# Block 2's adaLN vectors in a two-block transformer kernel: from GpSimd's products and sums to TensorE's column tiles

## The chip, the cores and the metric

The kernel runs on one core of one Trainium2 chip. The metric is the time of the whole program on the device, in microseconds (us): the median of three runs. Weights lie in HBM and are streamed to SBUF during the run; all data are fp32, some products run in fp32r halves or fp16.

## The reference

Two transformer blocks on 256 tokens of 1024 features. Block 1 ends in a layer of product-key experts ("PEER": 16384 experts in 128 rows of 128, each with a key `expert_u` and a value `expert_v`); block 2 has two layers, the second with routed experts. Each layer of block 2 starts from vectors that depend on the condition `c_2` alone:

```python
for l in range(DEPTH_2):                              # 2 layers
    mod = jax.nn.silu(c) @ ada_w[l] + ada_b[l]        # [1, 1024] @ [1024, 6144]
    sh1, sc1, g1, sh2, sc2, g2 = jnp.split(mod[:, None, :], 6, axis=-1)
    h = rmsnorm(x, ln1_g[l]) * (1.0 + sc1) + sh1
    ...
```

So 2 x 1024 x 6144 weights (48 MB) are read once and multiplied by one vector. In block 1 the experts' half computes, for every row of 128 experts, gelu(keys x h), times a weight for each expert and token (zero for those not chosen), times the values.

## The kernel before, in words

The kernel is one Python class `B`; its methods emit instructions in a program order, many as generators whose steps are woven together. The tile framework then puts them in order for each engine (by priority in program order, with a simulated timeline) and adds the waits; each engine and SP's queue then follow that order.

**The weights' stream.** `Ring` (L65) holds slots of 1 MB; a slot's DMA is issued on SP's queue as soon as the slot's last reader has been emitted (L98, and L96 for keys that come as four sources). `split` (L274 to 288) makes two fp32r halves of a weight tile: ScalarE copies the high one `whi` (L284), VectorE subtracts for `wlo` (L288). `mm3` (L404 to 409) is three TensorE products of such halves.

**The expert rows.** `peer` (L1327) works through 128 rows. T: the row's keys transposed, from row 32 on by VectorE (`peer_tv`, L1246: transposes L1254, ScalarE's copy `uth` L1255, VectorE's subtraction `utl` L1256). A: keys times h, 24 products of 256 columns (`peer_a`, L1295), gelu on ScalarE (L1301). W: the weights of the next group of 32 rows, a 32nd part beside each row (`peer_w_steps`, L1195): VectorE makes masks O2, eq, O1 (L1207 to 1209), TensorE eight small products (L1217), ScalarE and VectorE put them into W (L1222, L1223). g: weights times gelu on VectorE (L1310), its high half gh on ScalarE (L1312) and the remainder gl on GpSimd (L1313). Y: values times g, twelve products of 512 columns (`peer_y`, L1318). The key products of rows 0 to 31 run ahead while the experts are chosen; rows 96 to 127 have no next W. In rows 0 to 6 `group_steps` (L1259) also lays h out anew with banks of PSUM tag t.

**adaLN.** `mods` is one tile [128, 512]: value 512 j + i of a group of 2048 is at partition 32 j + r, column i, where r is the row of the group. Block 1's three groups come from `ada_steps` (L308): for each of eight chunks of 128 weight rows (1 MB, [128, 2048]) four products, one for each j, of a [128, 32] stationary operand that is zero but for one silu column, into partitions 32 j to 32 j + 31 of a PSUM bank. The zero columns put the sums into row r alone. Groups 1 and 2 go through `aring`, a ring with one slot. After eight chunks VectorE adds the bank to `mods` (L318).

Block 2's six groups come from `ada2_steps` (L321), in 96 steps of half a MB: 256 columns and half of the 1024 weight rows, into one half of a tile [128, 2, 4, 256] in the same slot as `aring`. On GpSimd: a product with the silu column (`c2`, L195; L348), two sums (L350; L352 and L353) into an accumulator `ada` (three buffers). When both halves are summed, TensorE multiplies the 256 columns by a column of ones (`pick`, L337), which sums over partitions; after eight such products VectorE adds the bank to `mods` (L340). The bank is of tag t, of which there are two.

**The order around it.** `self.ada(1)` (L1408) advances `ada2_steps` by one step in every second row of rows 0 to 31 and in each row after them; a step's DMA waits for GpSimd's work on the half before last. Rows 97, 104, 109 and 116 also emit the constants of block 2 and, at row 116, `prep2`, which reads the first of the new vectors. Banks of PSUM: four of tag acc (the sums Y), two of w, two of t.

Of the kernel before, what the change touches and what calls it, by code (L numbers as in the profile page):

```python
# [27 lines left out]
# block 2: chunks of w_in (z) and w_out (w), and the steps beside them  # L28
# [36 lines left out]
class Ring:  # L65
    """Slots of 1 MB that the weights stream through in the order of their use."""
# [6 lines left out]
    def grow(self, pool, n, tag="ring", until=None):  # L73
        """n more slots, for the entries before number until."""
        for _ in range(n):
            self.free.append((pool, n, tag, until))
        self._issue()

    def add(self, key, view, shape):
        """view: the source, or a list of sources for 32 partitions each with the first of them."""  # L80
        self.plan.append((key, view, shape))
# [21 lines left out]
    start = _issue  # L103
# [8 lines left out]
    def done(self):  # L112
        """The last instruction that reads the slot taken longest ago has been emitted."""
        self.free.append(self.inflight.popleft())
        self._issue()


def kchunk(w, k0, nk, c0, ncol):
    """Rows k0*128.. of a matrix [rows, cols] as [128, nk, ncol]."""
    return w[k0 * 128:(k0 + nk) * 128, c0:c0 + ncol].rearrange("(k p) c -> p k c", p=128)  # L120


class B:
# [27 lines left out]
    def splits(self, cx, n):  # L151
        """n more buffers for the parts of split weights while cx is open."""
        p = cx.enter_context(self.pool("split"))
        self.sps = self.sps + [(p, n)] * n
        cx.callback(self.unsplit, p)
# [4 lines left out]
    def rings(self, cx, n, until=None):  # L160
        """n more slots of the weights' ring, for the entries before number until."""
# [7 lines left out]
    # vectors laid as rows of 128, transposed to columns  # L169
# [18 lines left out]
    def vectors_T(self):  # L188
# [6 lines left out]
        self.c2 = self.cp.tile([128, 8], F32, name="c2")       # silu(c_2)  # L195
        nc.scalar.activation(self.c2, c2, AF.Sigmoid)
        nc.vector.tensor_tensor(self.c2, self.c2, c2, op=ALU.mult)
# [15 lines left out]
    def ln_stats(self, x, name="ln"):  # L213
        """mean and rstd of the rows of [128, 1024]."""
# [9 lines left out]
    def ln_norm(self, dst, x):  # L224
        """dst = (x - mean) * rstd."""
# [5 lines left out]
    def rms_norm(self, dst, x, g=None):  # L231
        """dst = x * rsqrt(mean of x^2 + eps) [* g]."""
# [13 lines left out]
    def modT_steps(self, *jobs):  # L246
        """For each job: hi/lo [128 d, 8, tok] = the transposed xn [128 tok, 2, 1024] * scale[d] + shift[d], in two parts.
        The first step needs xn alone."""
# [23 lines left out]
    def split(self, src, shape, tag="w", eng=None):  # L272
        """src as an fp32r high part and the fp32r rest."""
# [18 lines left out]
    # Value 512 j + i of a group of 2048 values is at partition 32 j + r, column i of mods, where r is the group's row:  # L292
    # 0..2 of block 1's three groups for the latent, 3 of the first for the context, 6 + 3 l + g in block 2.
# [12 lines left out]
    def ada_steps(self, g):  # L306
        """mods += the products of block 1's vectors with a group's weights; one step per 1 MB."""
# [13 lines left out]
    def ada2_steps(self):  # L321
        """The same for block 2, 256 columns and half of the rows a step: GpSimd sums over the rows that share a partition."""
        nc = self.nc
        parts = [(l, g, c, a) for l in range(2) for g in range(3) for c in range(8) for a in range(2)]
        slots = self.prep_pool.tile([128, 2, 4, 256], F32, tag="aring", name="ada2")
        accs, p = {}, None
        for n in range(len(parts) + 5):
            if n < len(parts):
                l, g, c, a = parts[n]
                nc.sync.dma_start(out=slots[:, n % 2], in_=kchunk(self.I["ada_w_2"][l], 4 * a, 4, 2048 * g + 256 * c, 256))  # L330
            if n % 2 == 0 and n >= 6:
                l, g, c, _ = parts[n - 6]
                r = 6 + 3 * l + g
                if p is None:
                    p = self.bank("t")
                j = 32 * (c // 2)
                nc.tensor.matmul(p[j:j + 32, 256 * (c % 2):256 * (c % 2) + 256], self.pick[:, 11 - r:43 - r], accs.pop(n // 2 - 3),  # L337
                                 start=True, stop=True)
                if c == 7:
                    nc.vector.tensor_tensor(self.mods, p, self.mods, op=ALU.add)  # L340
                    p = None
            if 1 <= n <= len(parts):
                i = n - 1
                w, a = slots[:, i % 2], i % 2
                if a == 0:
                    accs[i // 2] = self.pp.tile([128, 256], F32, tag="ada", name="ada", bufs=3)
                acc = accs[i // 2]
                nc.gpsimd.tensor_tensor(w, w, bcast(self.c2[:, 4 * a:4 * a + 4].rearrange("p (k o) -> p k o", o=1), (128, 4, 256)),  # L348
                                        op=ALU.mult)
                nc.gpsimd.tensor_tensor(w[:, 0:2], w[:, 0:2], w[:, 2:4], op=ALU.add)  # L350
                if a:
                    nc.gpsimd.tensor_tensor(acc, acc, w[:, 0], op=ALU.add)  # L352
                nc.gpsimd.tensor_tensor(acc, acc if a else w[:, 0], w[:, 1], op=ALU.add)  # L353
            yield
# [5 lines left out]
    def silu_cols(self):  # L360
        """silu of c and c_ctx as columns 2 and 5 of cs1, the rest zero."""
# [13 lines left out]
        self.pick = self.cp.tile([128, 43], F32, name="pick")     # ones in column 11  # L375
# [6 lines left out]
    def mod_cols(self, dst, r0, n, tag="t"):  # L382
        """dst [128, n, 16]: columns of the groups r0.. ."""
# [7 lines left out]
    def row_bcast(self, dst, r, js, scale=1.0, tag="t"):  # L391
        """dst [128, 512 * len(js)]: values 512 j.. of group r on every partition."""
# [11 lines left out]
    def mm3(self, o, ah, al, bh, bl, start, stop):  # L404
        """o += (ah + al)^T (bh + bl) without the product of the two rests."""
# [5 lines left out]
    def mm3u(self, o, wh, wl, kk, n):  # L411
        """mm3 with the first n of u's tokens (latent, then context); the first product clears the whole bank's marks."""
# [7 lines left out]
    def proj_steps(self, c0, n, res):  # L420
        """Features on partitions: res[ct] = [128 features, n tokens] of the 2 column tiles."""
# [14 lines left out]
    def projT_steps(self, c0, res, order=((0, (0, 1, 2, 3)), (1, (0, 1, 2, 3)))):  # L436
        """Tokens on partitions: res[tt] = [128 tokens, 256 features] of the 4 token tiles; order is the steps'
        half of the features that are summed over and token tiles."""
# [18 lines left out]
    def proj_lr(self):  # L457
        """The two gate ranks: partitions 96.. of a bank [128, 512 tokens]."""
# [8 lines left out]
    def hg_bounds(self):  # L467
        """max(lb, floor) and 1 - lb as columns [128, (direction, head)]."""
# [16 lines left out]
    def hg_gate(self, d, pr, banks):  # L485
        """Keys and decays of the latent and the context, [128, 2, 256] each."""
# [21 lines left out]
    def gla_gates(self, lr):  # L508
        """exp(logsigmoid / 16) of both directions: latent and context decays [128, 2, 256]."""
# [24 lines left out]
    def ctx_state(self, hpp, d, kc, fc, vc, res, rest=1):  # L534
        """End state [128 (dk of both groups' heads), 2, 128 dv] of the context in direction d."""
        nc = self.nc
        E = self.mt("E", (2, 256), 2)
        if d == 0:     # products of the later decays, by doubled blocks
# [15 lines left out]
        else:          # products of the earlier decays  # L554
# [22 lines left out]
        S = self.mt(f"S{d}", (2, 2, 128), 2)   # [dk of both heads, g, r, dv], zero where dk is the other head's  # L577
# [8 lines left out]
    # In blocks of 2 h tokens, the forward direction's keys of the first half meet the queries of the second half, the  # L586
    # backward direction's keys of the second half the queries of the first. A: a key's decays up to the halves' border;
    # P: a query's from the border. One doubling of h extends both by the other half's whole decay.
    def level_arrays(self, h, q, ks, A, P):
        """X of both directions [128, 2, 256]: keys times A in one half of each block, queries times P in the other."""  # L590
# [29 lines left out]
    def mix_steps(self, hpp, q, ks, fs, v, S, res):  # L620
        """o of the batch's heads in two banks of [128 tokens, heads x 128]."""
# [4 lines left out]
        Psb = self.mt("Psb", (4, 512))     # index 2 r + g for head hpp g + r  # L626
# [98 lines left out]
        # head norms  # L725
# [17 lines left out]
    def mix_out(self, o, h0, base, permuted, gain, gates):  # L743
        """Gain and gate; features base.. of the transposed mix in two parts, from heads h0, h0 + 1 of o."""
# [40 lines left out]
    def block1_mix(self, after):  # L785
        """The mixed tokens times w_out, in 4 banks; after(banks) runs while the mixer's memory is still held."""
        nc, I, tc = self.nc, self.I, self.tc
        O = self.WIN
        with ExitStack() as cx:
# [44 lines left out]
            back = []      # context states under way  # L834
# [43 lines left out]
            # the second mixer's parts  # L878
# [71 lines left out]
    def wout_steps(self, key, hi, lo, res):  # L950
        """[256 tokens, 1024] = (hi + lo)^T w in 4 banks (token tile, column half); the last chunk token tile by tile."""
# [1344 lines left out]
```

## Time and profile before

| | |
|---|---|
| time, median of 3 runs (all) | 2951.28 us (2951.82, 2949.05, 2951.28) |
| profiled execution: span on the core | 2951.2 us (no separate time for it) |
| mean granted TensorE clock | 0.950 |
| PE busy | 2671.7 us (91%) |
| VectorE (DVE) busy | 2475.4 us (84%) |
| ScalarE (ACT) busy | 1558.4 us (53%) |
| GpSimd (POOL) busy | 1006.3 us (34%) |
| HBM read | 616.18 MB, 209 GB/s over the span |

PE is TensorE's products, PEld its weight loads, SP the queue that issues most DMAs. L12 is line 12 of the kernel. An fp32 product shows as two records, each of the product's columns. A busy PE is not PE at its peak: the end of a product is modelled and a record overlaps the next; the pitch from start to start is what a product takes from the engine. The granted clock is a share of full speed (2.4 GHz is 1.0).

### The profile page before, as it was taken

To read this page: it belongs to the slowest core of one execution; us is meant where nothing else is said; L and a number is where in the kernel's file an instruction comes from. 1 tells how busy PE (TensorE), PEld (TensorE's weight loads), DVE (VectorE), ACT (ScalarE), POOL (GpSimd) and SP (SyncE) were. 2 spreads that over 40 slices of the span, in tenths; PEclk is the share of its full clock that TensorE was granted. 3 is DMA by queue.
4 is the path that set the end of the run, shared out by engine and by line. 5 is a ranking of instruction groups with operands and counts; after the bars stand their busy time and mean duration, and the time that the engine had idled before them with its cause. 6 is when DMAs were issued, how large, how long until landed. Compare 5 with 4: busy or idle time off the path is not lost. (4 is left out here: it accounts for less than half of the span.)

```text
span 2951.2 us, 45631 instructions
## 1 busy us (share of the span) xinstructions
PE 2671.7 (91%) x17417; PEld 2278.4 (77%) x17417; DVE 2475.4 (84%) x3850; ACT 1558.4 (53%) x2296; POOL 1006.3 (34%) x818
## 2 busy tenths in 40 slices
PE   6999796978898888888988899998999999999997
PEld 4878686956677777767877899987878778777775
DVE  4668799999899999999766754576999999999987
ACT  3244453433333333335446544475777777777775
POOL 2564353577677778776211100010000000000010
PEclk8999898989889999999998999998999999999999
DMA  7543442234666666667753455435999999999993
GB/s 256 199 147 102 152 138 84 101 107 157 179 182 170 189 171 193 178 181 203 184 182 104 133 179 180 142 126 178 348 338 352 339 342 350 335 344 342 338 333 146
DMA packets 341733, 620.28 MB, mean 210 GB/s; under 512 B 14755, under 2 KB 184633, under 8 KB 338433
## 3 DMA queue, kind: packets, MB, share of 16 engines
q1 hardware_dynamic: 340256, 616.06, 63.6%
q8 instruction: 138, 2.26, 0.3%
q0 software_dynamic: 1072, 0.82, 0.1%
q14 instruction: 91, 0.74, 0.1%
q10 hardware_dynamic: 176, 0.40, 0.0%
HBM read 616.18 MB, written 1.05 MB: 209 GB/s over the span
## 5 line engine op out<-in xcount | busy, mean ns | idle before, releaser
L288 DVE TENSOR_TENSOR wlo<-ring,whi 128x1024 fp32r<-128x1024 f32 x785 | 1027.1, 1329 | 235.9 <-ACT whi L284 230.5
L284 ACT ACTIVATE whi<-ring 128x1024 fp32r<-128x1024 f32 x785 | 822.6, 1058 | 520.2 <-PE acc L409 171.7
L2190 POOL TENSOR_TENSOR x<-x,moeroom 128x512 f32<-128x512 f32 x30 | 53.8, 1809 | 848.2 <-DVE moeroom L2189 848.2
L408 PE MATMUL acc<-wlo,xh 128*128 128x512 f32 x768 | 307.8, 401 | 2.8 <-DVE wlo L288 2.6
L407 PE MATMUL w<-hh,uth 128*128 128x256 f32 x1024 | 305.2, 298 | 4.4 <-DVE W L1223 1.4
L409 PE MATMUL acc<-whi,xl 128*128 128x512 f32 x768 | 304.0, 396 | 0.2 <-DVE xl L2133 0.2
L409 PE MATMUL w<-hh,utl 128*128 128x256 f32 x1024 | 300.7, 294 | 3.1 <-POOL utl L1243 3.1
L407 PE MATMUL acc<-whi,xh 128*128 128x512 f32 x768 | 301.4, 399 | 0.7 <-ACT xh L2132 0.7
L408 PE MATMUL w<-hl,uth 128*128 128x256 f32 x1024 | 298.9, 292 | 0.0
L348 POOL TENSOR_TENSOR ada<-ada,c 128x1024 f32<-128x1024 f32 x96 | 210.6, 2197 | 99.6 <-DMA ada<-in_ada_w_dram 99.4
L408 PE MATMUL acc<-wlo,gh 128*128 128x512 f32 x512 | 208.8, 418 | 25.7 <-DVE wlo L288 25.7
L407 PEld LDWEIGHTS w<-hh,uth 128*128 128x128 f32 x1024 | 204.7, 200 | 16.4 <-issue 3.1
L407 PE MATMUL acc<-whi,gh 128*128 128x512 f32 x512 | 192.0, 413 | 26.9 <-ACT gh L1312 26.8
L1256 DVE TENSOR_TENSOR utl<-ut,uth 128x512 fp32r<-128x512 f32 x192 | 188.3, 1016 | 28.2 <-ACT uth L1255 28.1
L409 PEld LDWEIGHTS w<-hh,utl 128*128 128x128 f32 x1024 | 203.5, 199 | 4.0 <-POOL utl L1243 3.8
L408 PEld LDWEIGHTS w<-hl,uth 128*128 128x128 f32 x1024 | 203.8, 199 | 3.1 <-issue 0.2
L409 PE MATMUL acc<-whi,gl 128*128 128x512 f32 x512 | 190.8, 433 | 9.3 <-POOL gl L1313 9.3
L1217 PEld LDWEIGHTS <-O 128*128 128x128 f16 x1024 | 117.5, 148 | 82.2 <-issue 48.9
L1255 ACT ACTIVATE uth<-ut 128x512 fp32r<-128x512 f32 x192 | 111.4, 622 | 128.5 <-PE w L408 86.6
L408 PEld LDWEIGHTS acc<-wlo,xh 128*128 128x128 f32 x768 | 144.6, 188 | 42.7 <-DVE wlo L288 7.6
L407 PEld LDWEIGHTS acc<-whi,xh 128*128 128x128 f32 x768 | 144.7, 188 | 35.4 <-ACT xh L2132 1.0
L409 PEld LDWEIGHTS acc<-whi,xl 128*128 128x128 f32 x768 | 144.6, 188 | 33.0 <-DVE xl L2133 0.6
(597 smaller groups left out, 6951.1 us busy)
## 6 DMA issues: line engine op xcount, KB each, us to landing
ring<-in_moe_w_gate_dram SPq DMA_DIRECT2D x79, 1024.0 KB, 6.0
ring<-in_moe_w_up_dram SPq DMA_DIRECT2D x79, 1024.0 KB, 6.3
ring<-in_moe_w_down_dram SPq DMA_DIRECT2D x78, 1024.0 KB, 5.8
ring<-in_peer_v_dram SPq DMA_DIRECT2D x64, 1024.0 KB, 5.3
ada<-in_ada_w_dram SPq DMA_DIRECT2D x96, 512.0 KB, 6.0
ring<-in_peer_u_dram SPq DMA_DIRECT2D x192, 256.0 KB, 4.9
ring<-in_w_in_dram SPq DMA_DIRECT2D x36, 1024.0 KB, 5.5
hT<-in_moe_w_down_dram SPq DMA_DIRECT2D x18, 1024.0 KB, 6.3
```

The costliest lines, as they stand in the source:

```text
L284: nc.scalar.activation(hv, src, AF.Copy)
L288: (eng or nc.vector).tensor_tensor(lv, src, hv, op=ALU.subtract)
L348: nc.gpsimd.tensor_tensor(w, w, bcast(self.c2[:, 4 * a:4 * a + 4].rearrange("p (k o) -> p k o", o=1), (128, 4, 256)), op=ALU.mult)
L407: mm(o, ah, bh, start=start, stop=False)
L408: mm(o, ah, bl, start=False, stop=False)
L409: return mm(o, al, bh, start=False, stop=stop)
L1217: nc.tensor.matmul(p[:, 64 * t:64 * t + 64], O2[:, :, t], O1[:, :, :, t], start=True, stop=True)
L1255: nc.scalar.activation(uh[:, b4], ut, AF.Copy)
L1256: nc.vector.tensor_tensor(ul[:, b4], ut, uh[:, b4], op=ALU.subtract)
L2190: (nc.vector if last and i > 1 else nc.gpsimd).tensor_tensor(self.x[:, t, c], self.x[:, t, c], tmp, op=ALU.add)
```

## The change

Block 2's vectors are made as block 1's are: `ada2_steps` loads 1 MB (128 weight rows, 2048 columns) into the one slot in a step, and in the next step issues four products with the padded silu column `cs2` into four column tiles of a bank. There are 48 such pairs of steps, 96 steps in all, driven by the same calls of `self.ada(1)`. The bank is taken at the first products of a group and held until its addition to `mods`. GpSimd's products and sums, the accumulators and the products with the ones' column go. `cs2` is a tile [128, 8, 43] with silu(c_2) in column 11 and zeros elsewhere. (The rest of the diff takes comments and docstrings out.)

```diff
-        self.c2 = self.cp.tile([128, 8], F32, name="c2")
-        nc.scalar.activation(self.c2, c2, AF.Sigmoid)
-        nc.vector.tensor_tensor(self.c2, self.c2, c2, op=ALU.mult)
+        self.cs2 = self.cp.tile([128, 8, 43], F32, name="cs2")
+        nc.gpsimd.memset(self.cs2, 0.0)
+        s2 = self.cp.tile([128, 8], F32, name="s2")
+        nc.scalar.activation(s2, c2, AF.Sigmoid)
+        nc.vector.tensor_tensor(self.cs2[:, :, 11], s2, c2, op=ALU.mult)
...
     def ada2_steps(self):
         nc = self.nc
-        parts = [(l, g, c, a) for l in range(2) for g in range(3) for c in range(8) for a in range(2)]
-        slots = self.prep_pool.tile([128, 2, 4, 256], F32, tag="aring", name="ada2")
...
-                nc.sync.dma_start(out=slots[:, n % 2], in_=kchunk(self.I["ada_w_2"][l], 4 * a, 4, 2048 * g + 256 * c, 256))
...
-                nc.tensor.matmul(p[j:j + 32, 256 * (c % 2):256 * (c % 2) + 256], self.pick[:, 11 - r:43 - r], accs.pop(n // 2 - 3),
-                                 start=True, stop=True)
...
-                nc.gpsimd.tensor_tensor(w, w, bcast(self.c2[:, 4 * a:4 * a + 4].rearrange("p (k o) -> p k o", o=1), (128, 4, 256)),
-                                        op=ALU.mult)
-                nc.gpsimd.tensor_tensor(w[:, 0:2], w[:, 0:2], w[:, 2:4], op=ALU.add)
-                if a:
-                    nc.gpsimd.tensor_tensor(acc, acc, w[:, 0], op=ALU.add)
-                nc.gpsimd.tensor_tensor(acc, acc if a else w[:, 0], w[:, 1], op=ALU.add)
-            yield
+        p = None
+        for l in range(2):
+            for g in range(3):
                 r = 6 + 3 * l + g
+                for k in range(8):
+                    w = self.prep_pool.tile([128, 2048], F32, tag="aring", name="ada2")
+                    nc.sync.dma_start(out=w, in_=self.I["ada_w_2"][l, k * 128:(k + 1) * 128, g * 2048:(g + 1) * 2048])
+                    yield
+                    if k == 0:
+                        p = self.bank("t")
+                    for j in range(4):
+                        nc.tensor.matmul(p[32 * j:32 * j + 32, :], self.cs2[:, k, 11 - r:43 - r], w[:, 512 * j:512 * (j + 1)],
+                                         start=(k == 0), stop=(k == 7))
+                    if k == 7:
+                        nc.vector.tensor_tensor(self.mods, p, self.mods, op=ALU.add)
+                    yield
```

## Rows read from the trace of the kernel before

**Rows 1.** Three stretches of expert rows (windows): busy us by engine, clock, DMA, GB/s.
```profile
608.00:790.00 182.00, 154.22 (x741) 117.42 (x741) 169.48 (x186) 61.48 (x110) 131.64 (x97) 0.89 0.52 156
790.00:1345.00 555.00, 486.04 (x2859) 406.64 (x2858) 549.07 (x650) 203.19 (x386) 423.29 (x288) 0.93 0.66 182
1345.00:1535.00 190.00, 181.38 (x1096) 158.63 (x1095) 144.96 (x209) 88.91 (x156) 75.89 (x59) 0.98 0.66 179
```

**Rows 2.** GpSimd's gl, one an expert row (one line): ns, first and last start.
```profile
L1313 POOL TENSOR_TENSOR gl<-g,gh x96: 727/1260/1807, 793.9 to 1531.3; 128x256 fp32r<-128x256 f32 x96
L1313 POOL TENSOR_TENSOR gl<-W,gh x32: 730/957/2236, 612.3 to 771.2; 128x256 fp32r<-128x256 f32 x32
```

**Rows 3.** VectorE's groups, 790 to 1345 us (lines): count, busy us, mean ns, idle.
```profile
L1256 DVE TENSOR_TENSOR utl<-ut,uth 128x512 fp32r<-128x512 f32 x126 | 134.6, 1105 | 1.2 <-ACT uth L1255 1.2
L288 DVE TENSOR_TENSOR wlo<-ring,whi 128x1024 fp32r<-128x1024 f32 x64 | 114.8, 1794 | 0.1
...
L1208 DVE TENSOR_TENSOR eq<-iotaT,i1T 128x256 f16<-128x256 f16 x60 | 53.6, 893 | 0.0
```

**Rows 4.** The mask eq over the whole span (source): min, median, max ns.
```profile
L1208 DVE TENSOR_TENSOR eq<-iotaT,i1T x128: 241/490/1984, 514.5 to 1318.0; 128x256 f16<-128x256 f16 x128
```

**Rows 5.** VectorE 900 to 918 us (timeline): start, us, line, then idle before.
```profile
904.01 2.91 DVE L288 TENSOR_TENSOR wlo<-ring,whi 128x1024 fp32r<-128x1024 f32 x1
...
913.01 1.21 DVE L288 TENSOR_TENSOR wlo<-ring,whi 128x1024 fp32r<-128x1024 f32 x1
...
914.34 1.28 DVE L1256 TENSOR_TENSOR utl<-ut,uth 128x512 fp32r<-128x512 f32 x2
```

**Rows 6.** GpSimd in the same stretch (timeline).
```profile
903.89 1.94 POOL L348 TENSOR_TENSOR ada<-ada,c 128x1024 f32<-128x1024 f32 x1
...
915.89 0.73 POOL L353 TENSOR_TENSOR ada<-ada 128x256 f32<-128x256 f32 x1 [3.42 <-PE t L337]
```

**Rows 7.** The adaLN instructions by stretch (windows, tile ada): PE, PEld, POOL.
```profile
608.00:790.00 182.00, 6.02 (x18) 1.28 (x18) 97.71 (x64) 0.89 0.52 156
790.00:1345.00 555.00, 21.14 (x64) 4.53 (x64) 356.15 (x224) 0.93 0.66 182
1345.00:1535.00 190.00, 2.48 (x8) 0.55 (x8) 31.76 (x22) 0.98 0.66 179
```

**Rows 8.** TensorE's waits in 790 to 1345 us (waits): us in all, times, longest.
```profile
PE w L1217 <- DVE W L1223: 32.2, 19, 3.5
PE acc L407 <- ACT gh L1312: 26.8, 17, 3.5
```

**Rows 9.** TensorE, one expert row from start to start at full clock (timeline).
```profile
921.25 0.39 PE L407 MATMUL acc<-whi,gh 128*128 128x512 f32 x1
...
925.05 0.28 PE L407 MATMUL w<-hh,uth 128*128 128x256 f32 x1
...
928.50 0.50 PE L407 MATMUL acc<-whi,gh 128*128 128x512 f32 x1 [0.42 <-ACT gh L1312]
```

**Rows 10.** Block 1's 1 MB adaLN step between projections on TensorE (timeline).
```profile
158.00 0.28 PE L417 MATMUL acc<-hl,whi 128*128 128x256 f32 x1
158.21 1.06 PE L314 MATMUL t<-aring,cs 128*32 128x512 f32 x8
...
159.43 0.28 PE L417 MATMUL acc<-hh,wlo 128*128 128x256 f32 x1
```

**Rows 11.** Block 2's adaLN product between other products on TensorE (timeline).
```profile
1454.12 0.40 PE L409 MATMUL acc<-whi,gl 128*128 128x512 f32 x1
1454.44 0.62 PE L337 MATMUL t<-ada,pick 128*32 128x256 f32 x2
...
1455.21 0.28 PE L408 MATMUL w<-hl,uth 128*128 128x256 f32 x1
```

**Rows 12.** Block 1's single 1 MB slot (tile aring): waits for it; landing.
```profile
  DMA aring<-in_w_ada_dram: 1.2, 3
...
DMA to landing us min/median/max: 4.9/5.0/13.4
```

More of the change, by code (lines that the diff above doesn't have):

```diff
@@ L323, in ada2_steps @@
         nc = self.nc
-        parts = [(l, g, c, a) for l in range(2) for g in range(3) for c in range(8) for a in range(2)]
-        slots = self.prep_pool.tile([128, 2, 4, 256], F32, tag="aring", name="ada2")
[L326 to L329, printed above, removed]
-                nc.sync.dma_start(out=slots[:, n % 2], in_=kchunk(self.I["ada_w_2"][l], 4 * a, 4, 2048 * g + 256 * c, 256))
-            if n % 2 == 0 and n >= 6:
-                l, g, c, _ = parts[n - 6]
-                r = 6 + 3 * l + g
-                if p is None:
-                    p = self.bank("t")
-                j = 32 * (c // 2)
-                nc.tensor.matmul(p[j:j + 32, 256 * (c % 2):256 * (c % 2) + 256], self.pick[:, 11 - r:43 - r], accs.pop(n // 2 - 3),
-                                 start=True, stop=True)
[L339 to L347, printed above, removed]
-                nc.gpsimd.tensor_tensor(w, w, bcast(self.c2[:, 4 * a:4 * a + 4].rearrange("p (k o) -> p k o", o=1), (128, 4, 256)),
-                                        op=ALU.mult)
-                nc.gpsimd.tensor_tensor(w[:, 0:2], w[:, 0:2], w[:, 2:4], op=ALU.add)
-                if a:
-                    nc.gpsimd.tensor_tensor(acc, acc, w[:, 0], op=ALU.add)
-                nc.gpsimd.tensor_tensor(acc, acc if a else w[:, 0], w[:, 1], op=ALU.add)
-            yield
```

## The prediction, made before the changed kernel was run

> **What bounds the kernel now.** I read the page's busy shares first, then the slices, then cut the stretch where block 2's adaLN work lies into three by the expert rows: GpSimd makes one remainder gl for each of the 128 rows, 32 of them (rows 0 to 31, whose key products were made ahead) from 612 to 771 us and 96 from 794 us on [rows 2]. So 608 to 790 us holds rows 0 to 31, 790 to 1345 us rows 32 to 95 (these build the next weights W too), 1345 to 1535 us rows 96 to 127. In the windows the reader sees VectorE busy 549 of 555 us in the middle stretch and 169 of 182 in the first, while TensorE has 486 and 154 at a mean clock of 0.93 and 0.89; in the last stretch it turns round: TensorE 181 of 190, VectorE 145 [rows 1]. A row of the middle stretch takes 555/64 = 8.7 us. VectorE sets that, and TensorE waits for it directly and through ScalarE: 32.2 us for W's sums, 26.8 us for gh, which ScalarE makes from VectorE's g [rows 8].
>
> VectorE is full because its work is stretched. The same subtraction wlo took 2.91 us at 904.01, when GpSimd ran adaLN products and sums back to back, and 1.21 us at 913.01, when GpSimd stood idle (its next instruction, at 915.89, had 3.42 us of idle time before it); two utl together took 1.28 us at 914.34 [rows 5, 6]. The means in the middle stretch are 1794 ns for wlo, 1105 ns for utl, 893 ns for the mask eq [rows 3]; eq's least is 241 ns, its greatest 1984 [rows 4], near a whole GpSimd product of 1.94 us [rows 6]. So an operation of VectorE with both inputs in SBUF waits until GpSimd's has ended. adaLN is 356 of GpSimd's 423 busy us in the middle stretch, 98 of 132 in the first, 32 of 76 in the last [rows 1, 7].
>
> **The change part by part.** *Removed: GpSimd's products and sums.* All of that work goes; what stays on GpSimd is mainly gl. Off VectorE come, in the middle stretch, at least 126 x (1.105 - 0.64) = 59 us for utl, 64 x (1.794 - 1.21) = 37 us for wlo, 60 x (0.893 - 0.241) = 39 us for eq [rows 3 to 5]. 549 - 135 = 414 us, 6.5 us a row, without counting what O and g gain, which are stretched in the same way; some collisions with gl stay.
>
> *What is late next: TensorE.* At full clock one row of the middle stretch, with no adaLN in it, runs from 921.25 to 928.50 us with 0.42 us of waiting: 6.83 us, of which 3.80 (to 925.05) are the sums Y and the weights W, the rest the key products [rows 9].
>
> *Removed: 48 products of GpSimd's sums with the ones' column.* From 1454.12 to 1455.21 us stand one 512-column product, the pair, and one 256-column product; less the usual pitch of 0.235 and 0.12 us of the two, a pair costs 0.74 us [rows 11].
>
> *Added: 48 groups of four column tiles.* Block 1 makes the same group of the same shapes, eight records for four products: from 158.00 to 159.43 us it stands with two neighbours of 0.12 us each, so a group costs 1.43 - 0.24 = 1.19 us, entry and exit included [rows 10]. The bounds of this price: 1.06, the records alone, and 1.43, the neighbours included. Net on TensorE: 48 x (1.19 - 0.74) = 22 us if nothing else moved. The steps are placed by the program order: 8 groups in rows 0 to 31, 32 in rows 32 to 95, 8 in rows 96 to 111 (the old pairs by records: 9, 32 and 4 [rows 7]).
>
> The group of eight records in 1.0 us is the point where a rule speaks against the change. The Trainium skill, FP8 and Floating Point Precision, section TensorE Precision Notes, says that a true FP32 product makes four passes through the array; an estimate from that page, four products of four passes of 512 columns one after the other at 2.4 GHz, is 3.4 us a group, and by it the sum below would be 48 x 2.2 = 106 us worse. No run here shows such a group: the row of block 1 has it in a third of that, so the sum goes by the row.
>
> *Transfers and SP's queue.* The bytes stay 48 MB; 96 issues of half a MB become 48 of 1 MB with rows of 8 KB in place of 1 KB, on the same SP queue between the loads of keys and values. The two half slots become one slot: SP's next adaLN load now waits for TensorE's group, and behind it in SP's queue stand the ring's loads, on which ScalarE's and VectorE's splits wait. The group waits on its load, and behind the group stands all of TensorE. Block 1 runs just this scheme, one slot, load, group, load: landing took 5.0 us (median) and TensorE waited 1.2 us in 16 steps [rows 12]. The program gives a group two expert rows, some 15 us, so I take 0.1 us a group, 4 us in all, and keep 0 and 48 x 2.5 = 120 us as ends (a landing of 13.4 us, the longest, at each step would show as far more than 1.2 us of waits in 16).
>
> *Small edits.* The padded silu column (a memset on GpSimd, one sigmoid, one strided product, once, before block 1's projections) costs nothing: it stands beside the wait for the first weights; uncovered it is some 1 us, by gl's 0.73 us for 256 elements [rows 2]. A PSUM bank of tag t is now held from row 3 on, not row 13, so the regrouping of h in rows 3 to 6 has one such bank: nothing if each row's turn covers a bank's round trip, at most 4 x 3.5 = 14 us by the longest wait here [rows 8]. The six additions to mods stay.
>
> *Sum.* Middle stretch: 64 x 6.83 + 32 x 1.19 = 475 us of TensorE; where TensorE is the bound today it is busy 181/190 = 0.955 [rows 1], so 475/0.955 = 497 us: -58. First stretch: 32 x 3.80 + 8 x 1.19 = 131 us, beside other work of at most 154 - 122 - 6 = 26 us [rows 1, 7, 9]; 157/0.955 = 165: -17; if half of that other work is only slow clock, 144/0.955 = 151 us: -31. I take -22, below halfway, as the rows there are short. Last stretch: 8 x 1.19 - 4 x 0.74 = +6. Waiting for loads: +4. Of the 96 old records 18 + 64 + 8 = 90 lie in the three stretches [rows 7], so a sixteenth of the work lies before 608 us, some 30 us of GpSimd; at the first stretch's 22 us for 98 that is -7, and I take -4, since VectorE need not be the bound there. Together -58 - 22 + 6 + 4 - 4 = -74. What follows (block 2, then the experts, transfers at their limit) starts earlier by as much and is unchanged. The profiled span is 2951.2 us, as good as the median 2951.28, and the page gives no separate time for it: 2951 - 74 = 2877 us.
>
> **The rivals.** *VectorE stays the bound.* In-order VectorE and TensorE, interleaved row by row, may not run together at 0.955, or gl (up to 2.2 us stretched [rows 2]) keeps colliding. For it: TensorE's waits are spread over many places. Against: 414 us of VectorE leave a quarter of the stretch free. Half of the gain is lost: 2951 - 74/2 = 2914 us. Chance 0.17.
>
> *TensorE waits for the single slot (the other side).* If the loads, behind ring loads in SP's queue, land late so that each group waits 2.5 us, it is 48 x 2.5 = 120 us on the bound engine: 2877 + 116 = 2993 us. It decides from 74/48 = 1.5 us a group. For it: one slot in place of two halves, in one queue with the ring. Against: the 16 steps of block 1 [rows 12]. Chance 0.08.
>
> *The four tiles run one after the other.* Then the change does not do what it says. The old pair takes 0.62 us for two records of 256 columns [rows 11], so 0.31 us each and 0.62 us for one of 512 columns; eight of them are 5.0 us a group, 48 x 3.8 = 182 us more: 3059 us. Chance 0.01, since block 1 shows 1.06 us [rows 10]. By the four passes of the Trainium skill's page FP8 and Floating Point Precision it would be 2877 + 106 = 2983 us.
>
> *More than forecast.* TensorE at its floor: 475 us in the middle (-80), -31 in the first stretch, -6 before it, no loss in the last: 2951 - 117 = 2834 us. Chance 0.1.
>
> **How the numbers follow.** Forecast 0.64, the two small gains and losses around it as above. The range goes from the floor, 2834, to somewhat beyond the half gain, 2925 us; about 0.18 lies outside. A measurement here can tell some 0.2%, 6 us, from no change. Faster: 0.64 + 0.10 + 0.14 of the second case = 0.88; same 0.03 (the rest of that case); slower 0.09.
>
> **What would show it.** Right: in 790 us and on, wlo near 1.25 us, eq under 0.5, GpSimd mainly gl; TensorE busy 95% at a clock near 1 with rows about 7.5 us apart; 384 records of the new products, a group near 1.2 us; its waits for the adaLN load under 10 us. Wrong: VectorE's means unchanged with GpSimd quiet; groups over 2 us; TensorE's longest waits on the adaLN load or on SP; or a gain in the rows that is given back in block 2.

## The result and the profile after

The changed kernel takes 2838.18 us (median; 2835.94 to 2840.83) against 2950.65 for the kernel before, run in turn with it: a ratio of 0.9619, 95% interval 0.9605 to 0.9633. That is 112 us less; the profiled span falls from 2951.2 to 2834.1 us, by 117. The forecast was 2877 us, a gain of 74 by the span: the right way and for the right reason, and a third too small, with the measured time 4 us above the lower end of the range (2834). The kernel before was timed again beside each experiment below; its medians lay between 2948.1 and 2950.7 us.

The windows of the expert rows in the changed kernel, rows 0 to 31 and rows 32 to 127, cut at the first and last remainder gl (columns as in [rows 1]):

```profile
601.20:753.20 152.00, 151.79 (x845) 110.73 (x842) 108.75 (x191) 59.93 (x111) 28.46 (x32) 0.99 0.68 226
753.20:1416.50 663.30, 658.14 (x4108) 545.62 (x4107) 480.51 (x852) 289.41 (x540) 131.17 (x101) 0.99 0.68 197
```

The same GpSimd line that [rows 2] shows, here L1300 (min/median/max ns, first and last start):

```profile
L1300 POOL TENSOR_TENSOR gl<-g,gh x96: 731/1467/1712, 753.2 to 1416.5; 128x256 fp32r<-128x256 f32 x96
L1300 POOL TENSOR_TENSOR gl<-W,gh x32: 731/742/2250, 601.2 to 731.7; 128x256 fp32r<-128x256 f32 x32
```

The reader is to see that the two engines have changed places. TensorE is busy 151.8 of 152.0 and 658 of 663 us at a clock of 0.99, where [rows 1] has waits and 0.89 to 0.98; VectorE, which was full, has a quarter of the time free; GpSimd works a fifth of it. From the first gl to the last the rows take 1416.5 - 601.2 = 815.3 us, before 1531.3 - 612.3 = 919.0.

VectorE's groups over all rows of the changed kernel (lines, by form: count, busy us, mean ns, idle before), which answer to [rows 3]:

```profile
L290 DVE TENSOR_TENSOR wlo<-ring,whi 128x1024 fp32r<-128x1024 f32 x125 | 152.5, 1220 | 26.6 <-ACT whi L286 26.4
...
L1243 DVE TENSOR_TENSOR utl<-ut,uth 128x512 fp32r<-128x512 f32 x192 | 127.3, 691 | 67.4 <-ACT uth L1242 67.4
...
L1195 DVE TENSOR_TENSOR eq<-iotaT,i1T 128x256 f16<-128x256 f16 x94 | 28.9, 308 | 0.2
```

wlo is at 1.22 us, utl at 0.69, eq at 0.31, near what [rows 4, 5] showed as their unhindered times. TensorE's waits in the same stretch, which answer to [rows 8], come to almost nothing:

```profile
PE t L337 <- DMA ada<-in_ada_w_dram: 5.0, 1, 5.0
PE w L394 <- ACT ga L1288: 0.4, 2, 0.2
```

What block 2's adaLN work now is (tile ada), and where it lies (windows of that tile: PE, PEld), answering to [rows 7, 12]:

```profile
L337 PE MATMUL t<-ada,cs x384: 592/616/1064, 584.2 to 1241.2; 128*32 128x512 f32 x192
L332 SPq DMA_DIRECT2D ada<-in_ada_w_dram x48: 327/352/412, 187.7 to 1231.6; - x48
...
  DMA ada<-in_ada_w_dram: 10.2, 2
...
DMA to landing us min/median/max: 5.0/5.5/11.4
```

```profile
601.20:753.20 152.00, 17.41 (x124) 2.49 (x120) 0.99 0.68 226
753.20:1241.40 488.20, 55.88 (x240) 7.77 (x240) 1.00 0.70 204
1241.40:1416.50 175.10, 0.84 (x4) 0.00 (x0) 0.99 0.63 177
```

384 records for 192 products, all inside the rows or just ahead of them, the last at 1241 us. With eight records to a group, three groups lie ahead of the rows (the last of them reaches into the first window), 15 in rows 0 to 31 and 30 in rows 32 to 95; the four records in the last stretch are the end of the group before. The program order gave 8, 32 and 8: the framework's order let the groups run ahead, as their loads and TensorE allowed. For a load TensorE waited once, 5 us by its own row in the waits.

By the same markers the gain lies as follows (us):

| stretch | before | after | change |
|---|---|---|---|
| up to the first gl | 612.3 | 601.2 | -11.1 |
| rows 0 to 31 (to the first gl of row 32) | 181.6 | 152.0 | -29.6 |
| rows 32 to 95 (to the last sum into W) | 551.8 | 488.2 | -63.6 |
| rows 96 to 127 (to the last gl) | 185.6 | 175.1 | -10.5 |
| after the rows | 1419.9 | 1417.6 | -2.3 |

(The last sum into W starts at 1345.7 us before and at 1241.4 after.) Nothing is given back behind the rows.

### The profile page after: what moved, and what is told of

Its sections match the earlier page's. It is cut to its first block, busy times and chain, and to the rows that moved or that the text cites. A ratio compares the mean times of both kernels' runs of the same rounds, so it can differ in the third digit from the quotient of the medians.

```text
span 2834.1 us, 45752 instructions
## 1 busy us (share of the span) xinstructions
PE 2664.2 (94%) x17705; PEld 2253.8 (80%) x17705; DVE 2194.2 (77%) x3850; ACT 1556.8 (55%) x2296; POOL 493.8 (17%) x483
## 5 line engine op out<-in xcount | busy, mean ns | idle before, releaser
L290 DVE TENSOR_TENSOR wlo<-ring,whi 128x1024 fp32r<-128x1024 f32 x785 | 968.6, 1254 | 246.0 <-ACT whi L286 240.1
L394 PE MATMUL w<-hh,uth 128*128 128x256 f32 x1024 | 296.8, 290 | 2.6 <-ACT W L1288 1.0
L396 PE MATMUL w<-hh,utl 128*128 128x256 f32 x1024 | 294.5, 288 | 3.1 <-POOL utl L1230 3.1
L395 PE MATMUL w<-hl,uth 128*128 128x256 f32 x1024 | 291.7, 285 | 0.0
L394 PEld LDWEIGHTS w<-hh,uth 128*128 128x128 f32 x1024 | 195.8, 191 | 33.5 <-issue 24.3
L1300 POOL TENSOR_TENSOR gl<-g,gh 128x256 fp32r<-128x256 f32 x96 | 128.4, 1338 | 534.2 <-ACT gh L1299 528.6
L396 PEld LDWEIGHTS w<-hh,utl 128*128 128x128 f32 x1024 | 195.5, 191 | 3.9 <-POOL utl L1230 3.8
L395 PEld LDWEIGHTS w<-hl,uth 128*128 128x128 f32 x1024 | 196.1, 192 | 2.5
L1194 DVE TENSOR_TENSOR O<-iotaT,i2T 128x1024 f16<-128x1024 f16 x128 | 96.2, 753 | 127.7 <-PE w L1204 121.2
L1243 DVE TENSOR_TENSOR utl<-ut,uth 128x512 fp32r<-128x512 f32 x192 | 127.3, 691 | 67.4 <-ACT uth L1242 67.4
```

The costliest lines, as they stand in the source:

```text
L290: (eng or nc.vector).tensor_tensor(lv, src, hv, op=ALU.subtract)
L394: mm(o, ah, bh, start=start, stop=False)
L395: mm(o, ah, bl, start=False, stop=False)
L396: return mm(o, al, bh, start=False, stop=stop)
L1194: nc.vector.tensor_tensor(O2, self.iotaT, bt(i2T[:, ts], 128), op=ALU.is_equal)
L1243: nc.vector.tensor_tensor(ul[:, b4], ut, uh[:, b4], op=ALU.subtract)
```

## The experiments

The theory: GpSimd's reads of SBUF stretched VectorE's operations, VectorE was the bound of the rows, and with the reads gone TensorE is, which now pays for the groups. Rivals: the gain comes from the loads' shape or the order of instructions; the groups cost nothing because they lie in idle time. All times below are medians; "rows" is the time from the first gl to the last.

**e1: GpSimd's reads put back.** Behind each group of the changed kernel:

```diff
+                    e = self.pp.tile([128, 512], F32, tag="ada", name="ada")
+                    nc.gpsimd.tensor_tensor(e, w[:, 0:512], w[:, 512:1024], op=ALU.add)
+                    for _ in range(7):
+                        nc.gpsimd.tensor_tensor(e, e, e, op=ALU.add)
```

> The changed kernel, with GpSimd work of about the removed size put back beside TensorE's groups: eight sums of 512 columns for each 1 MB, 48 x 8 x 1.3 = 500 us, that read SBUF and whose result nothing uses. Theory (VectorE's operations with two SBUF inputs wait for GpSimd's reads; their removal is the gain): wlo and utl are stretched again to over 1.5 and 1.0 us on average in the expert rows, VectorE is full, and the time goes back to 2930 to 2975 us. Rival (the gain comes from the loads' shape and the fewer issues on SP's queue, or from the new order of instructions): 2838 us, at most 10 more.

Measured: 2929.95 us, ratio to the kernel before 0.9948 (0.9917 to 0.9979), so 92 us of the 112 are lost again, at the very lower end of what the theory gave. VectorE in the rows (lines, by form):

```profile
L1247 DVE TENSOR_TENSOR utl<-ut,uth 128x512 fp32r<-128x512 f32 x192 | 217.4, 1161 | 26.9 <-ACT uth L1246 24.8 <-PE w L400 2.0
L290 DVE TENSOR_TENSOR wlo<-ring,whi 128x1024 fp32r<-128x1024 f32 x125 | 203.9, 1631 | 14.8 <-ACT whi L286 14.5
...
L1199 DVE TENSOR_TENSOR eq<-iotaT,i1T 128x256 f16<-128x256 f16 x94 | 54.1, 575 | 0.2
```

TensorE's waits there, and rows 32 to 95 (windows):

```profile
PE w L1208 <- DVE W L1214: 30.0, 26, 2.8
PE acc L399 <- DVE wlo L290: 9.9, 8, 2.7
```

```profile
771.40:1325.00 553.60, 518.94 (x3045) 403.84 (x3043) 542.99 (x654) 200.40 (x383) 400.19 (x308) 0.97 0.60 183
```

wlo and utl are stretched as before, and in rows 32 to 95, where 65 of the 92 us are lost, VectorE is the bound again (543 of 554 us); TensorE waits for W's sums and for wlo. The edit also changes the order of instructions: the 48 groups stand in 91 pieces on TensorE, in the changed kernel in 72 (see e4). In the last rows, where TensorE is busy 183 of 188 us, that and the groups that now lie there may be part of the loss; it was not separated. eq suffers less than in the kernel before (0.58 against 0.89 us), perhaps since a sum of 512 columns is shorter than a product of 1024; that was not tried.

**e2: GpSimd writes alone.**

```diff
+                    for a in range(6):
+                        nc.gpsimd.memset(w[:, 1024 * (a % 2):1024 * (a % 2) + 1024], 0.0)
```

> The changed kernel, with GpSimd busy by writes alone: six memsets of 1024 columns into the slot after each group, 48 x 6 x 0.95 = 270 us. If it is the reads that collide: wlo stays under 1.3 us on average, 2838 to 2850 us. If any work of GpSimd stretches VectorE: half of the old stretch, wlo near 1.5 us, and with VectorE's slack 2850 to 2895 us.

Measured: 2824.95 us, ratio 0.9578 (0.9550 to 0.9606), 13 us faster than the changed kernel (the two intervals just touch), which no theory had. The lines of the rows (by form):

```profile
L342 POOL MEMSET ada<- 128x1024 f32 x282 | 257.1, 957 | 116.7 <-PE t L337 97.6 <-issue 9.7 <-POOL gl L1302 9.4
...
L290 DVE TENSOR_TENSOR wlo<-ring,whi 128x1024 fp32r<-128x1024 f32 x125 | 171.5, 1372 | 24.8 <-ACT whi L286 24.7
...
L1245 DVE TENSOR_TENSOR utl<-ut,uth 128x512 fp32r<-128x512 f32 x192 | 127.5, 702 | 88.1 <-ACT uth L1244 85.2 <-PE w L398 2.8
...
L1197 DVE TENSOR_TENSOR eq<-iotaT,i1T 128x256 f16<-128x256 f16 x94 | 28.4, 302 | 0.1
```

257 us of memsets leave utl and eq where they were without them (0.70 and 0.30 us). wlo is at 1.37, not under 1.3 as expected; but in e8 below, without a memset, it is at 1.40:

```profile
L290 DVE TENSOR_TENSOR wlo<-ring,whi 128x1024 fp32r<-128x1024 f32 x125 | 175.5, 1404 | 20.0 <-ACT whi L286 19.8
```

So it needs no writes. Where wlo is longer, GpSimd's gl is shorter: 1.22 and 1.47 us (gl's median over rows 32 to 127) in the changed kernel, 1.37 and 0.86 in e2, 1.40 and 0.86 in e8. Both read two tiles of SBUF, so it is likely that they hold up one another; no run tries it. The Trainium skill, SBUF — State Buffer, section Who interferes with whom, says that a VectorE instruction with two SBUF inputs collides with a GpSimd instruction that reads SBUF and not with one that only writes it. The trace of e1 agrees with the first half by wlo and utl (1.63 and 1.16 us), that of e2 with the second by utl and eq.

Why e2 is faster than the changed kernel e4 and e7 show: its groups are whole on TensorE. It keeps 13 of the 34 us that this gives in e7, for it loses some 24 us against e7 in rows 96 to 127 (windows of e2):

```profile
1209.80:1404.40 194.60, 187.14 (x1160) 156.35 (x1159) 126.86 (x204) 87.98 (x157) 100.53 (x101) 0.97 0.74 214
```

In e7 they take 170.7 us. A load has to wait for the memsets in its slot, and ten groups were left for these rows.

**e3: the kernel before without GpSimd's work.** 

```diff
-                nc.gpsimd.tensor_tensor(w, w, ..., op=ALU.mult)
...
-                nc.tensor.matmul(p[...], self.pick[:, 11 - r:43 - r], accs.pop(n // 2 - 3), start=True, stop=True)
+                for a in range(2):
+                    nc.tensor.matmul(p[...], self.pick[:, 11 - r:43 - r], slots[:, a, 0], start=(a == 0), stop=(a == 1))
```

> The kernel before without GpSimd's products and sums: the half-MB loads of 1 KB rows stay, TensorE multiplies a quarter of each half by the ones' column (so block 2's vectors are not what the reference computes). Theory: the whole gain and more, since TensorE's groups are not there: 2838 less 48 x 0.2 to 0.45 us, 2815 to 2830 us. Rival (loads' shape, order): near 2951 us.

Measured: 2822.0 us, ratio 0.9568 (0.9540 to 0.9596), in the range of the theory. Its windows:

```profile
603.50:766.50 163.00, 157.69 (x790) 114.32 (x789) 104.66 (x189) 59.75 (x109) 25.66 (x32) 0.97 0.74 226
766.50:1403.90 637.40, 634.30 (x3977) 545.20 (x3977) 485.87 (x852) 289.08 (x540) 120.25 (x101) 1.00 0.72 199
```

With the loads of before and no GpSimd products, TensorE is full at once (634 of 637 us). The gain is GpSimd's silence, not the shape of the loads or the groups.

**e4: a small product for each group.**

```diff
-                    for j in range(4):
-                        nc.tensor.matmul(p[32 * j:32 * j + 32, :], self.cs2[:, k, 11 - r:43 - r], w[:, 512 * j:512 * (j + 1)],
-                                         start=(k == 0), stop=(k == 7))
+                    nc.tensor.matmul(p[0:32, 0:8], self.cs2[:, k, 11 - r:43 - r], w[:, 0:8], start=(k == 0), stop=(k == 7))
```

> The changed kernel with one product of 8 columns in place of each group of four of 512 (block 2's vectors are left out but for the bias): the loads and their pace stay. If TensorE is now the bound and a group costs what it takes in the row, 48 x (1.19 - 0.2) = 48 us: 2790 us. If the groups lie in TensorE's idle time: 2838 us.

Measured: 2777.73 us, ratio 0.9418 (0.9391 to 0.9445): 60 us less than the changed kernel, more than the 48 expected. Its windows, and one small product among its neighbours on TensorE (timeline):

```profile
603.10:749.40 146.30, 142.53 (x755) 113.87 (x756) 105.97 (x191) 60.14 (x111) 26.98 (x33) 0.96 0.73 244
749.40:1361.00 611.60, 608.16 (x3924) 538.49 (x3923) 502.67 (x852) 286.57 (x540) 101.27 (x100) 1.00 0.71 211
```

```profile
907.54 0.28 PE L394 MATMUL w<-hh,utl 128*128 128x256 f32 x1
907.75 0.23 PE L336 MATMUL t<-ada,cs 128*32 128x8 f32 x2
907.91 0.50 PE L392 MATMUL acc<-whi,gh 128*128 128x512 f32 x1
908.25 0.40 PE L393 MATMUL acc<-wlo,gh 128*128 128x512 f32 x1
```

The rows take 1361.0 - 603.1 = 757.9 us, 57 less than with the groups: the groups do not lie in idle time of TensorE. A small product costs 908.25 - 907.54 less the neighbours' 0.12 and 0.235, 0.35 us. If 48 groups cost 1.19 each, the difference should have been 48 x 0.84 = 40 us, and some 2 less here, as TensorE is idle 7 us in e4's rows and 5 in the changed kernel's. So a group in the changed kernel costs more than the one in [rows 10]. Its timeline on TensorE shows why:

```profile
865.43 0.28 PE L396 MATMUL w<-hh,utl 128*128 128x256 f32 x1
865.63 1.04 PE L337 MATMUL t<-ada,cs 128*32 128x512 f32 x2
866.61 1.16 PE L1204 MATMUL w<-O,O 128*128 128x64 f16 x8
...
870.18 0.40 PE L396 MATMUL acc<-whi,gl 128*128 128x512 f32 x1
870.51 1.06 PE L337 MATMUL t<-ada,cs 128*32 128x512 f32 x6
871.50 0.39 PE L394 MATMUL w<-hh,uth 128*128 128x256 f32 x1
```

The group is split. The framework's order puts one product (two records) at 865.63 us and the other three (six records) at 870.51, with eight small products of W and twelve products of the sums Y between them; the lone one takes 0.98 us to the next start, the three 0.99. In the trace 23 of the 48 groups are split so and one into two and two, which makes 72 turns of 48. In e2 nearly all are whole (47 of 48), at the same price a turn (1.00 us).

**e5: loads in rows of 1 KB.**

```diff
-                    nc.sync.dma_start(out=w, in_=self.I["ada_w_2"][l, k * 128:(k + 1) * 128, g * 2048:(g + 1) * 2048])
+                    nc.sync.dma_start(out=w.rearrange("p (k c) -> p k c", k=8),
+                                      in_=kchunk(self.I["ada_w_2"][l], 0, 8, 2048 * g + 256 * k, 256))
```

> The changed kernel with its 1 MB loads in pieces of 1 KB, as the kernel before read them (256 columns of all 1024 rows, so the products meet other weights and block 2's vectors are not the reference's). Theory (the loads' shape is no part of the gain as long as TensorE does not wait for them): 2838 us, within 6. Rival (8 KB pieces land sooner and free the transfers): 2850 to 2880 us, with waits of TensorE for the load.

Measured: 4139.2 us, ratio 1.403 (1.4007 to 1.4054). That says nothing of the loads: with other vectors an expert got more tokens than it has places, and the kernel ran its branch for the rest of them (tile over):

```profile
L290 DVE TENSOR_TENSOR wlo<-over,whi 128x1024 fp32r<-128x1024 f32 x576 | 689.7, 1235 | 361.1 <-ACT whi L286 359.4 <-PE acc L397 1.0
```

Up to the end of the rows the comparison holds, by the gl lines:

```profile
L1301 POOL TENSOR_TENSOR gl<-g,gh x96: 732/1468/1713, 754.1 to 1415.6; 128x256 fp32r<-128x256 f32 x96
L1301 POOL TENSOR_TENSOR gl<-W,gh x32: 731/744/2243, 601.3 to 732.6; 128x256 fp32r<-128x256 f32 x32
```

They end at 1415.6 us, in the changed kernel at 1416.5: the shape of the loads is worth nothing here. (Landing took 6.0 us in the median, against 5.5.)

**e6: two of the six groups of vectors while the experts are chosen.**

```diff
-                        p = self.bank("t")
+                        p = self.bank("acc" if 3 * l + g < 2 else "t")
...
+                calls = 32
                 for _ in self.choose(*top, pick):
                     run_ahead(1)
+                    self.ada(min(calls, 2))
+                    calls -= min(calls, 2)
+                self.ada(calls)
```

> The changed kernel with two of the six groups of vectors (16 MB, 16 groups of products) made while the experts are chosen, in a PSUM bank of tag acc, where VectorE is the bound and TensorE has idle time. If TensorE bounds the expert rows and has room while the experts are chosen: 16 x 1.19 = 19 us less, 2815 to 2825 us. Rival (the groups delay the key products there, or the rows wait elsewhere): 2838 us or more.

Measured: 2807.29 us, ratio 0.9523 (0.9507 to 0.9539): 31 us less than the changed kernel, where 13 to 23 were expected. The stretch in which the experts are chosen, in the changed kernel and in e6 (windows):

```profile
390.00:540.00 150.00, 119.77 (x933) 116.34 (x932) 142.71 (x817) 73.16 (x146) 70.78 (x67) 0.90 0.27 93
```

```profile
390.00:540.00 150.00, 130.62 (x1016) 111.11 (x1015) 141.08 (x808) 70.77 (x139) 66.72 (x64) 0.94 0.58 202
```

TensorE takes up the 16 groups there (11 us more busy, at a higher clock), and the rows start 7 us later but take 36 us less, 779.4. In its order only 14 groups are split, not 24. By the prices so far, 16 groups at 1.19 us and ten turns fewer at about as much are 31 of the 36 us.

**e7: the groups kept together.** The changed kernel with one line more, around the four products:

```diff
+                    with self.tc.high_priority():
```

> The changed kernel with the four products of a group kept together on TensorE (high priority for them), where the changed kernel's order splits 24 of the 48 into two parts with other products between. If each part costs a whole group's turn (parts of one, three and four products took 0.98, 0.99 and 1.00 us from start to next start): 24 turns less, 0.6 to 1.0 us each, 14 to 24 us: 2814 to 2824 us. Rival (a single product between others is cheaper, or fills idle time): 2838 us.

Measured: 2804.16 us, ratio 0.9507 (0.9493 to 0.9520), 34 us less than the changed kernel and more than the 14 to 24 expected. The timeline of a group, and the gl lines:

```profile
876.86 0.28 PE L397 MATMUL w<-hh,utl 128*128 128x256 f32 x1
877.07 1.06 PE L338 MATMUL t<-ada,cs 128*32 128x512 f32 x8
878.07 0.51 PE L395 MATMUL acc<-whi,gh 128*128 128x512 f32 x1
```

```profile
L1301 POOL TENSOR_TENSOR gl<-g,gh x96: 733/1208/1739, 752.9 to 1387.5; 128x256 fp32r<-128x256 f32 x96
L1301 POOL TENSOR_TENSOR gl<-W,gh x32: 736/742/1979, 604.0 to 735.0; 128x256 fp32r<-128x256 f32 x32
```

Eight records take 1.00 us from start to next start, two took 0.98. The rows take 1387.5 - 604.0 = 783.5 us, 31.8 less than in the changed kernel; 24 turns at the full 1.19 us of [rows 10] are 28.6, and TensorE's busy time in the rows falls by 809.9 - 782.0 = 27.9 us, 1.16 a turn. The expectation was low because it left entry and exit out of a part's price, and e7 also has no wait for a load.

That puts e4 in order: of its 57 us in the rows some 28 were the extra turns. Against e7, with whole groups, e4's rows are 25.6 us shorter, where 45 groups at 0.84 would be 38. In e4's rows TensorE is idle 7.2 us (e7 1.5), and its first stretch has a clock of 0.96 (e7 0.99); how much of the missing 12 us that is was not tried.

**e8 and e9: whole, and two or three of the six groups of vectors early.** e8 has the edits of e6 and e7; e9 changes e8's 2 to 3 and 32 calls to 48, three in a step.

> e6 with the products kept together as in e7. e6's order split 14 of the 48, so 14 turns of 0.6 to 1.0 us less than e6's 2807 us: 2793 to 2799 us. Rival: no change from 2807 us.

> e8 with three of the six groups of vectors made while the experts are chosen. If TensorE has still room there: 8 x 0.9 = 7 us less than e8, about 2788 us. Rival (the third one delays the key products and the start of the rows, and that costs what the rows gain): e8's time or more.

Measured: e8 2792.78 us, ratio 0.9470 (0.9456 to 0.9484), at the lower end of the range (2793); e9 2797.64 us, ratio 0.9487 (0.9473 to 0.9500). The gl lines of e8, then of e9:

```profile
L1301 POOL TENSOR_TENSOR gl<-g,gh x96: 732/856/1543, 758.0 to 1374.2; 128x256 fp32r<-128x256 f32 x96
L1301 POOL TENSOR_TENSOR gl<-W,gh x32: 732/742/2241, 608.3 to 740.2; 128x256 fp32r<-128x256 f32 x32
```

```profile
L1301 POOL TENSOR_TENSOR gl<-g,gh x96: 735/854/1532, 771.2 to 1379.7; 128x256 fp32r<-128x256 f32 x96
L1301 POOL TENSOR_TENSOR gl<-W,gh x32: 736/742/2243, 621.8 to 753.1; 128x256 fp32r<-128x256 f32 x32
```

The rival holds for e9: its rows are 8 us shorter (757.9 against 765.9) and start 13.5 us later. Making the third group of vectors early costs more ahead of the rows than it saves in them; what delays them there was not looked into. e8 is the best version found, 45 us under the changed kernel and 155 us under the kernel before.

## Why the prediction was right, and where its size was off

*What bounds.* Right. VectorE set the rows up to 95, by GpSimd's reads: e1 brings the bound back, e3 removes it from the kernel before.

*What is late next.* Right: TensorE, in all rows, with VectorE under three quarters. The prices hold: a turn more costs 1.16 us (e7) where 1.19 was taken, and with whole groups rows 32 to 95 take (463.9 - 29 x 1.19)/64 = 6.71 us a row beside their 29 groups, where 6.83 was taken. In e7 (windows):

```profile
752.90:1216.80 463.90, 462.82 (x3052) 389.56 (x3050) 361.69 (x654) 204.30 (x390) 75.82 (x69) 1.00 0.72 214
```

*The step that failed: dividing TensorE's work by 0.955.* That share came from 1345 to 1535 us of the kernel before. All of the 8.6 us that TensorE lost there lie before 1400 us, where GpSimd's last adaLN sums end (the last starts at 1399.2); behind that it was full in the kernel before already (windows of the kernel before):

```profile
1400.00:1535.00 135.00, 135.00 (x828) 119.39 (x828) 89.99 (x134) 62.09 (x111) 35.88 (x30) 0.99 0.64 174
```

In the changed kernel TensorE is busy 809.9 of 815.3 us, 0.993, so the term should have been near the floor that the prediction kept for its range. For rows 32 to 95 it gave 497 us; 488 were measured, although 23 of the 24 split groups lie there. With whole groups (e7) these rows take 463.9 us, so the term was 33 us too long. For rows 0 to 31 the prediction took 160 us; 152 were measured with 15 groups instead of 8.

*The last rows: +6 forecast, -10.5 measured.* Two errors in one term. The groups were placed by the program order; they ran ahead of it, and none was left for rows 96 to 127. And GpSimd's work there was named (32 of 76 us [rows 7]) but its stretch of VectorE, and the 8.6 us that TensorE waits there, were not counted.

*Before the rows: -4 forecast, -11.1 measured.* The prediction took GpSimd's share there from TensorE's old products, a sixteenth of them, some 30 us, and counted it at about half its price. GpSimd ran ahead of those products; the trace of the kernel before has 42.5 us of its adaLN work there (windows of tile ada: PE, PEld, POOL):

```profile
186.00:608.00 422.00, 1.92 (x6) 0.55 (x6) 42.47 (x27) 0.90 0.33 109
```

At the first stretch's 22 us for 98 that is 9.5 us. About half of the 11.1 us is there when VectorE's first sum into W starts (521.7 us before, 516.3 after).

*Loads and the single slot: +4 forecast, one wait of 5 us measured.* Right, by the scheme's own model in block 1 [rows 12].

*Not foreseen: the split groups.* The prediction took a group as one block, as block 1 has it. Half of them are not, and pay entry, exit and a full turn twice: 28 us of TensorE's time in the rows, and whole groups make the rows 32 us shorter (e7). It hid the size of the first error, and that is luck: the span missed by 43 us (117 against 74), with whole groups (e7's span of 2806.8 us) it would have been 70. Of the 43 the last rows make 16.5, rows 32 to 95 with the wait for loads 9.6, rows 0 to 31 7.6, what lies before the rows 7.1 and what lies behind them 2.3.

*The rule weighed in the prediction.* The Trainium skill, FP8 and Floating Point Precision, section TensorE Precision Notes, has four passes for a true FP32 product, estimated from it as 0.85 us for one of 512 columns. The lone product of the split groups is near that, with 0.98 us to the next start. Four in column tiles took 1.00 us in e7, so they run beside one another, and the sum went by the right row.

*The rivals.* VectorE as the remaining bound, the wait for the slot and the tiles one after the other did not come. "More than forecast", TensorE at its floor, 2834 us with chance 0.1, is nearest in time and has the mechanism right. That its gain of 117 us is the measured one is luck: it has 80 us for rows 32 to 95, where 63.6 came, 6 before the rows, where 11.1 came, and nothing for the last rows, where 10.5 came.

## What to carry to other kernels

GpSimd work that reads SBUF is not free beside a full VectorE, however idle GpSimd is: count what it adds to each VectorE operation with two SBUF inputs, and compare with TensorE's price for the same sums. When the engine that was stretched is no longer the bound, take the next engine's work at its unhindered pitch, not at a share read where the old bound still showed. Column tiles are worth their price only side by side: look in the order of instructions whether a scheduler has split the group.

## What the runs showed of the hardware

A turn in column tiles of 32 columns took the same time for one, three and four fp32 products of 512 columns: 0.98, 0.99 and 1.00 us from start to next start, and 0.2 us more by the neighbours' later starts. Memsets of 1024 columns on GpSimd (0.957 us each) left VectorE's utl and eq at 0.70 and 0.30 us, while sums of 512 columns stretched utl from 0.69 to 1.16 and wlo from 1.22 to 1.63 us on average.
